# A one-core transformer layer in fp32: no tensor arithmetic on GpSimd, one-hot rows built four tokens at a time, and another order for the last layer norm

## The chip, the cores and the metric

The kernel runs on one core of a Trainium2 chip. The metric is the device time of one execution in microseconds; three runs of the kernel before gave 4892.66, 4898.55 and 4910.54 us, so the median is 4898.55 us. One further execution was recorded by the hardware profiler, and all views below come from it.

A core has five engines with instruction queues of their own: TensorE (PE; its weight loads are listed apart as PEld), VectorE (DVE), ScalarE (ACT), GpSimd (POOL) and SyncE (SP). SP computes nothing and issues transfers; ACT and POOL issue some too. Each engine works through its queue in order.

## The reference

One layer for 512 tokens of width 2048, in fp32, with three sublayers, each followed by `layer_norm(2**0.25 * x + h)`:

```
h = hybrid_mixer(x)              # mLSTM (4 heads) and forgetting attention (16 heads), gated and merged
x = layer_norm(DN_ALPHA * x + h, ln_w[0], ln_b[0])
h = memory_cross_attention(x, mem)
x = layer_norm(DN_ALPHA * x + h, ln_w[1], ln_b[1])
h = peer_ffn(x)                  # 8 heads, 16 of 16384 experts each
x = layer_norm(DN_ALPHA * x + h, ln_w[2], ln_b[2])
```

The expert sublayer matters here:

```
q = (x @ w_pq)                              # per head two halves of 128
sc = einsum(q, sub_keys)                    # 128 scores for each half
top_s, top_i = top_k(sc, 16)                # per half
cand_s = top_s[0][:, None] + top_s[1]       # 256 sums
cand_i = top_i[0][:, None] * 128 + top_i[1]
best_s, best_pos = top_k(cand_s, 16)
idx = cand_i[best_pos];  g = softmax(best_s)
a = expert_u[idx] . x                       # 128 experts per token
out = sum(gelu(a) * g * expert_v[idx])
```

## The kernel before

Every fp32 matrix product is made of three products of a split operand: a number is cast to a high half that TensorE takes at its fast fp32 rate (`hi`, by ScalarE) and the remainder (`lo = x - hi`). `split` (line 133) does this; `load_pair` (line 155) loads a weight tile of 128x1024 through SP and splits it, and `mm3`/`products` issue hi*hi, hi*lo and lo*hi. The subtraction for the low half is on VectorE, except that `load_w` (line 180) counts its loads and gives every eighth one (`work["share"] = 8`; every third one during the first sixteen steps) to GpSimd until the gates are built.

The 512 tokens go in two paths: block 0 alone (path A), then blocks 1 to 3 together (path B, 384 columns). Path A's stages run first, interleaved with other products by `weave`. The work of the expert sublayer is done in two ways. For the first 128 tokens and the last 96 tokens the chosen rows of `expert_u` and `expert_v` are fetched by indirect transfers that GpSimd issues (`gathered`), multiplied and summed by VectorE, a few steps at a time beside other stages. For the 288 tokens between them (`NDENSE`) all 16384 experts are computed densely in 128 chunks of 128 experts: `stage_a(c)` makes the chunk's activations for 288 tokens and applies gelu, `stage_h(c)` multiplies them by the chunk's gates and splits the result, and `stage_o(c0, q)` multiplies eight chunks by a quarter of `expert_v`'s columns and adds the result to an accumulator `acc` held with features on the partitions.

The gates of the dense part are a table: for each token and expert the softmax weight, or zero. It is built (lines 1245 to 1269) as a product of one-hot rows: for a token, `o1` holds a row for each of its 128 picks with a one at the second index, `o0` the same for the first index scaled by the weight, and one matmul of the two gives the token's 128x128 gates. Four tokens share a PSUM bank. ScalarE copies a bank into staging tiles (five buffers), and for each 48 tokens four transfers store these to DRAM (`gd`). `stage_h` needs the whole table. While it is built, TensorE also runs `stage_a` for the first 76 chunks (`LOOK`); most of their results wait in DRAM (`gad`).

Before the gates comes the selection (`select`, 16 calls): repeated max, index search and replacement on VectorE, with one sum and two products of 128x512 on GpSimd.

`norm` (line 743) normalises a path's rows, transposes them, applies weight and bias per feature, splits the result for the next products, transposes it back and stores it as `x2d`. The last layer norm is in `fin` (line 978): for each block of rows, statistics, then the first 1024 columns with two VectorE instructions and the other 1024 with ScalarE, GpSimd and VectorE in turn, then a store. For the dense tokens the accumulator is transposed back in quarters at the end of `stage_o`, and `2**0.25 * x` is added there from three row tiles loaded from `x2d`.

The order of the instructions on each engine, and the interleaving of independent stages on TensorE, is not written by hand: a planner lays it out when the kernel is built, from the program's order and its own estimates of durations. Rings of buffers (`bufs=`) limit how far a producer runs ahead. `after(i, other)` adds a wait to hold gathers back.

## Time and profile before

| | |
|---|---|
| median of three runs | 4898.55 us |
| profiled execution | 4901.6 us, its span 4899.9 us |
| granted TensorE clock, mean | 0.985 |
| PE busy | 4707.2 us (96%), 28705 matmuls |
| PE weight load busy | 4347.4 us (89%) |
| DVE busy | 3736.8 us (76%) |
| ACT busy | 2130.8 us (43%) |
| POOL busy | 1345.5 us (27%) |
| DMA | 1433.60 MB, mean 293 GB/s |

How to read the views: a line such as `L137 DVE TENSOR_TENSOR wlo<-raw,whi` names the line of the kernel, the engine, the operation, and what it writes from what. Where a helper issues an instruction the line is the helper's. `SPq`, `ACTq` and `POOLq` are instructions of the engine's queue that only issue or wait. A trailing `[7.94 <-DMA G<-gd]` means that the engine was idle for 7.94 us before, and that the landing of that transfer ended it. A matmul's busy time overlaps that of its neighbours, so busy sums of groups exceed the time that passes; busy time by stretch doesn't count an overlap twice.

The stages in time: path A and the products woven into it up to about 1600 us; path B's mixer, attention and cross attention up to about 2940 us; path B's last norm of this part around 2941 to 2964 us; queries and selection up to 3365 us, with `stage_a` from 3104 us; the gates from 3365 to 3661 us; the output products from 3686 to 4873 us; the last norm up to 4900 us.

### The profile page before, as it was taken

How to read it: one execution, taken by the hardware profiler on the slowest of the kernel's cores; microseconds unless marked ns; L12 is line 12 of the kernel's file. 1: busy time of each engine (PE TensorE's matmuls, PEld its weight loads, DVE VectorE, ACT ScalarE, POOL GpSimd, SP SyncE). 2: the span in 40 equal slices, each digit the busy share in tenths (PEclk: the TensorE clock that was granted, in tenths of full speed). 3: DMA queues.
4: the chain of work that ended last, by engine and by line, in shares of the span. 5: the costliest groups of instructions: out<-in, count | busy, mean ns of one | idle time of the engine just before them, and what ended most of it. 6: DMA issues, size and time to landing. Idle time of an engine off the chain costs nothing. (4 is left out here: it accounts for less than half of the span.)

```text
span 4899.9 us, 75254 instructions
## 1 busy us (share of the span) xinstructions
PE 4707.2 (96%) x28705; PEld 4347.4 (89%) x28705; DVE 3736.8 (76%) x5360; ACT 2130.8 (43%) x3108; POOL 1345.5 (27%) x1058
## 2 busy tenths in 40 slices
PE   7999999999999899999989999999998999999997
PEld 6888778878888899999988779999998999999997
DVE  7776666765698776887768585899877878888886
ACT  6665666555643322343332334434443433343333
POOL 2122222311124444434444232231111222221111
PEclk9999999999999999999999999999999999999999
DMA  7888888866559898998889584588788989989994
GB/s 259 277 290 281 290 321 311 281 226 200 193 188 357 332 358 338 342 334 328 301 297 381 192 298 164 205 281 281 282 290 325 347 339 350 345 332 348 359 336 146
DMA packets 380026, 1433.60 MB, mean 293 GB/s; under 512 B 43852, under 2 KB 104908, under 8 KB 320624
## 3 DMA queue, kind: packets, MB, share of 16 engines
q1 hardware_dynamic: 266208, 831.34, 47.9%
q0 software_dynamic: 91712, 559.45, 30.4%
q10 hardware_dynamic: 21744, 38.02, 2.1%
q8 instruction: 224, 3.67, 0.3%
q14 instruction: 138, 1.13, 0.1%
HBM read 1339.13 MB, written 89.40 MB: 292 GB/s over the span
## 5 line engine op out<-in xcount | busy, mean ns | idle before, releaser
L134 ACT CAST whi<-raw 128x1024 fp32r<-128x1024 f32 x1472 | 1526.1, 1051 | 1769.0 <-PE mm L208 780.0
L137 DVE TENSOR_TENSOR wlo<-raw,whi 128x1024 fp32r<-128x1024 f32 x1349 | 1690.3, 1265 | 711.5 <-ACT whi L134 496.2
L905 POOL DMA_INDIRECT rows<-in_peer_u,eid x224 | 327.4, 1462 | 994.6 <-DVE rows L933 352.0
L905 POOL DMA_INDIRECT rows<-in_peer_v,eid x224 | 367.4, 1640 | 837.6 <-DVE xacc L936 437.1
L208 PE MATMUL po<-hph,whi 128*128 128x288 f32 x2048 | 553.4, 297 | 33.7 <-ACT hph L134 19.5
L933 DVE SCALAR_TENSOR_TENSOR rows<-rows,xacc 128x2048 f32<-128x2048 f32 x224 | 528.0, 2361 | 71.6 <-DMA rows<-in_peer_u,eid 71.1
L936 DVE SCALAR_TENSOR_TENSOR xacc<-rows,dots,xacc 128x2048 f32<-128x2048 f32 x224 | 540.8, 2414 | 42.9 <-DMA rows<-in_peer_v,eid 41.5
L208 PE MATMUL sm<-Ch,whi 128*128 128x288 f32 x2048 | 561.3, 298 | 2.3 <-ACT whi L134 1.3
L208 PE MATMUL sm<-Cl,whi 128*128 128x288 f32 x2048 | 559.1, 297 | 0.0
L208 PE MATMUL po<-hpl,whi 128*128 128x288 f32 x2048 | 553.2, 297 | 1.9 <-DVE hpl L137 1.9
L136 POOL TENSOR_TENSOR wlo<-raw,whi 128x1024 fp32r<-128x1024 f32 x123 | 315.7, 2567 | 714.9 <-ACT whi L134 407.4
L208 PE MATMUL mm<-xh,whi 128*128 128x384 f32 x1280 | 436.7, 343 | 6.5 <-ACT sg L575 2.7
L208 PE MATMUL mm<-xl,whi 128*128 128x384 f32 x1280 | 429.4, 337 | 0.0
L208 PEld LDWEIGHTS po<-hph,whi 128*128 128x128 f32 x2048 | 385.0, 190 | 36.8 <-ACT hph L134 19.7
L208 PEld LDWEIGHTS sm<-Ch,whi 128*128 128x128 f32 x2048 | 385.4, 188 | 4.0 <-ACT whi L134 2.4
L208 PEld LDWEIGHTS po<-hpl,whi 128*128 128x128 f32 x2048 | 385.1, 190 | 3.8 <-DVE hpl L137 2.1
L208 PEld LDWEIGHTS sm<-Cl,whi 128*128 128x128 f32 x2048 | 385.6, 188 | 0.0
L208 PE MATMUL po<-hph,wlo 128*128 128x288 f32 x2048 | 339.3, 296 | 2.0 <-DVE wlo L137 2.0
L208 PE MATMUL sm<-Ch,wlo 128*128 128x288 f32 x2048 | 320.6, 297 | 0.4 <-DVE wlo L137 0.4
L208 PEld LDWEIGHTS po<-hph,wlo 128*128 128x128 f32 x2048 | 295.1, 189 | 5.2 <-DVE wlo L137 3.5
L208 PEld LDWEIGHTS sm<-Ch,wlo 128*128 128x128 f32 x2048 | 287.7, 188 | 2.4 <-DVE hpl L137 0.8
L208 PE MATMUL mm<-xh,wlo 128*128 128x384 f32 x1280 | 255.4, 335 | 0.0
(430 smaller groups left out, 8832.7 us busy)
## 6 DMA issues: line engine op xcount, KB each, us to landing
raw<-in_w_in SPq DMA_DIRECT2D x512, 512.0 KB
raw<-in_uT SPq DMA_DIRECT2D x256, 512.0 KB
raw<-in_vq SPq DMA_DIRECT2D x256, 512.0 KB
raw<-in_w_xkv SPq DMA_DIRECT2D x64, 512.0 KB
raw<-in_w_br_ml SPq DMA_DIRECT2D x64, 512.0 KB
raw<-in_w_br_fx SPq DMA_DIRECT2D x64, 512.0 KB
raw<-in_w_out SPq DMA_DIRECT2D x64, 512.0 KB
raw<-in_peer_wq SPq DMA_DIRECT2D x64, 512.0 KB
```

The source lines that it names most:

```text
L134: nc.scalar.copy(hi, src)
L136: return nc.gpsimd.tensor_sub(lo, src, hi.bitcast(F32))
L137: return nc.vector.tensor_sub(lo, src, hi.bitcast(F32))
L208: nc.tensor.matmul(o, w if stat else x, x if stat else w, start=k == first and x is xh and not part, stop=k == last and part == 1)
L905: i = nc.gpsimd.indirect_dma_start(out=rows, out_offset=None, in_=I[table], in_offset=bass.IndirectOffsetOnAxis(ap=ei[:, k:k + 1], axis=0))
L933: after(nc.vector.scalar_tensor_tensor(rows, rows, 1.0, xacc, op0=ALU.mult, op1=ALU.mult, accum_out=dots[:, k:k + 1]), last())
L936: after(nc.vector.scalar_tensor_tensor(xacc, rows, dots[:, k:k + 1], xacc, op0=ALU.mult, op1=ALU.add), last())
```

## The change

1. GpSimd computes no tensors. The low halves that it made (`share`) go to VectorE, as do the sum and the two products in `select`, and the product in `fin`, whose second 1024 columns now take the same two VectorE instructions as the first. GpSimd keeps issuing transfers and gathers.
2. Gates: both one-hot tiles are made for four tokens by one VectorE comparison each (128x512), with two buffers each; the scaling by the weight is done in place by ScalarE, one instruction of 128x128 per token.
3. `norm` for path B's second norm also stores its transposed output (288 columns of each of 16 feature tiles) to a new array `x2td`, with transfers issued from ScalarE. During the output products, each of the 16 tiles is loaded back once by SP into the ring of `gb` and added, times `2**0.25`, to the accumulator. The three row tiles of `x2d` are no longer loaded at the end.
4. The last norm of the dense tokens: after each quarter the statistics are taken from the transposed bank, and the bank is multiplied by the weight row into `yw`. At the end the root is taken for the three row tiles together. The remaining part, weight times -mean*rstd plus bias, comes from a matmul with five rows (the split weight row against the split factor, and the split bias row against ones), and one VectorE instruction per quarter and tile adds it to `yw * rstd`. Stores go out from SP and ScalarE.

```diff
-        def split(hi, lo, src, pool=False):
+        def split(hi, lo, src):
             nc.scalar.copy(hi, src)
-            if pool:
-                return nc.gpsimd.tensor_sub(lo, src, hi.bitcast(F32))
             return nc.vector.tensor_sub(lo, src, hi.bitcast(F32))
...
         def load_w(src):
-            work["n"] += 1
-            pool = work["share"] and work["n"] % work["share"] == 0
-            hi, lo, i = load_pair(src, pool)
-            if not pool:
-                work["last"] = i
+            hi, lo, work["last"] = load_pair(src)
...
                     i_last = split(*o[-1], f)
+                    if keep is not None:
+                        nc.scalar.dma_start(keep[c], f[:, :NDENSE])
...
-            nc.gpsimd.tensor_tensor(cand, vv[:, :, 0].unsqueeze(3).to_broadcast(full),
+            nc.vector.tensor_tensor(cand, vv[:, :, 0].unsqueeze(3).to_broadcast(full),
...
-                nc.gpsimd.tensor_mul(eq, eq, ii[:, :, q].unsqueeze(2).to_broadcast(full))
+                nc.vector.tensor_mul(eq, eq, ii[:, :, q].unsqueeze(2).to_broadcast(full))
...
-                o1 = gp.tile([P, 4, P], F32, tag="o1", bufs=2, name=nm("o1"))
-                nc.vector.tensor_tensor(o1, iota.unsqueeze(1).to_broadcast([P, 4, P]),
-                                        selT["i1"][:, ta:ta + 4].unsqueeze(2).to_broadcast([P, 4, P]),
-                                        op=ALU.is_equal)
+                o0, o1 = (gp.tile([P, 4, P], F32, tag=f"o{k}", bufs=2, name=nm("o")) for k in (0, 1))
+                for o, k in ((o0, "i0"), (o1, "i1")):
+                    nc.vector.tensor_tensor(o, iota.unsqueeze(1).to_broadcast([P, 4, P]),
+                                            selT[k][:, ta:ta + 4].unsqueeze(2).to_broadcast([P, 4, P]),
+                                            op=ALU.is_equal)
                 for u in range(4):
                     c = slice(ta + u, ta + u + 1)
-                    o0 = gp.tile([P, P], F32, tag="o0", bufs=4, name=nm("o0"))
-                    nc.vector.tensor_scalar(o0, iota, selT["i0"][:, c], selT["g"][:, c],
-                                            op0=ALU.is_equal, op1=ALU.mult)
-                    nc.tensor.matmul(bank[:, u * P:(u + 1) * P], o1[:, u], o0, start=True, stop=True)
+                    nc.scalar.activation(o0[:, u], o0[:, u], AF.Copy, scale=selT["g"][:, c])
+                    nc.tensor.matmul(bank[:, u * P:(u + 1) * P], o1[:, u], o0[:, u], start=True, stop=True)
...
+        def weighted(t, q, bank):
+            n, sl = size(t), slice(q * 512, (q + 1) * 512)
+            i = nc.vector.tensor_mul(yw[t][:n, sl], bank[:n], last_norm["w"][:n, sl])
+            after(i, last_norm.get("aggr"))
...
+                nc.vector.bn_stats(st[:n, t, 6 * q:6 * q + 6], bank[:n])
+                if q < 3:
+                    weighted(t, q, bank)
+                else:
+                    last_norm["aggr"] = nc.vector.bn_aggr(st[:n, t, 24:26], st[:n, t, 0:24])
+                    rest.append(bank)
...
+            rstd(st[:, :, 26], st[:, :, 25], (st[:, :, 28], st[:, :, 29]))
+            nc.vector.scalar_tensor_tensor(st[:, :, 27], st[:, :, 24], -1.0, st[:, :, 26], op0=ALU.mult, op1=ALU.mult)
+            for k in (2, 3):
+                nc.vector.tensor_copy(cs5[:, :, k], st[:, :, 27])
+            nc.vector.tensor_sub(cs5[:, :, 4], st[:, :, 27], cs5[:, :, 2].bitcast(F32))
...
+            nc.scalar.copy(l5[:5, :NDENSE], tb[:5, :NDENSE])
+            for t in range(NT):
+                weighted(t, 3, rest[t])
+            for t in range(NT):
+                n = size(t)
+                for q in range(4):
+                    sl = slice(q * 512, (q + 1) * 512)
+                    bank = sm_bank()
+                    nc.tensor.matmul(bank[:n], l5[:5, t * P:t * P + n], rw[:5, sl], start=True, stop=True)
+                    o = yw[t][:n, sl]
+                    nc.vector.scalar_tensor_tensor(o, o, st[:n, t, 26:27], bank[:n], op0=ALU.mult, op1=ALU.add)
...
-                lwd.extend(fin_load(gat))
-                for t in range(NT):
-                    n = min(P, NDENSE - t * P)
-                    xr[t] = gp2.tile([P, D], F32, tag=f"xr{t}", name=f"xr{t}")
-                    nc.gpsimd.dma_start(xr[t][:n], x2d[t + 1, :n].rearrange("p g c -> p (g c)"))
+                columns_load()
...
+            k = c0 // J
+            if 1 <= k <= 8 and q < 2:
+                b = 2 * (k - 1) + q
+                xt = mn.tile([P, NDENSE], F32, tag="gb", bufs=4, name=nm("xt"))
+                nc.sync.dma_start(xt, x2td[b])
+                nc.vector.scalar_tensor_tensor(acc[:, b], xt, ALPHA, acc[:, b], op0=ALU.mult, op1=ALU.add)
```

`columns_load` loads the weight row broadcast to all partitions, and weight and bias as single rows, splits these two and copies the halves into the five rows of `rw`, all from GpSimd's queue, when the last group of chunks begins.

More of the change, by code (lines that the diff above doesn't have):

```diff
@@ L34 @@
 GB = 48
-SHARE = 8
 NEG = -1.0e30
@@ L1013, in build @@
         A, B = Path(0, 1, XA), Path(1, 3, XB)
-        work["share"] = SHARE
         with tc.tile_pool(name="sa", bufs=1, side="right", reuse_waits="tile") as sa:
@@ L1231, in build @@
                 soften(tp, sel[t]["g"])
-        work["share"] = 0
         def o_bank(i=0):
@@ new lines, in size, with turned_out @@
+        def size(t):
+            return min(P, NDENSE - t * P)
+        def weighted(t, q, bank):
+            n, sl = size(t), slice(q * 512, (q + 1) * 512)
+            i = nc.vector.tensor_mul(yw[t][:n, sl], bank[:n], last_norm["w"][:n, sl])
+            after(i, last_norm.get("aggr"))
+        def turned_out(q):
+            st, rest = last_norm["st"], []
+            for t in range(NT):
+                n = size(t)
+                bank = o_bank()
+                for s in range(4):
+                    nc.tensor.transpose(bank[:n, s * P:(s + 1) * P], acc[:, 4 * q + s, t * P:t * P + n], ident)
+                nc.vector.bn_stats(st[:n, t, 6 * q:6 * q + 6], bank[:n])
[4 more added lines that the diff above has]
+                    rest.append(bank)
+            return rest
```

68 lines of the change are left out of this document (42 added, 26 removed).

## The prediction, made before the change was run

> **What bounds the kernel now.** I read the page's first lines, then busy time by stretch, then what TensorE waited for, then the timelines around its longest waits and at the end. In the stretch view the columns are the length and then the busy time of PE, its weight load, DVE, ACT and POOL, each with its instruction count, then the granted TensorE clock, the DMA share and GB/s.
>
> ```profile
> PE 4707.2 (96%) x28705; PEld 4347.4 (89%) x28705; DVE 3736.8 (76%) x5360; ACT 2130.8 (43%) x3108; POOL 1345.5 (27%) x1058
> ```
> ```profile
> 100.00:1600.00 1500.00, 1456.28 (x7686) 1239.67 (x7684) 1053.21 (x1626) 842.55 (x1158) 380.34 (x344) 0.99 0.77 268
> 1600.00:2900.00 1300.00, 1256.48 (x6630) 1155.87 (x6631) 986.87 (x1039) 432.93 (x629) 525.56 (x401) 0.98 0.86 322
> 2941.00:2964.00 23.00, 20.50 (x125) 18.99 (x126) 16.05 (x31) 21.56 (x42) 5.45 (x11) 0.80 0.26 104
> 3100.00:3365.00 265.00, 259.49 (x1941) 258.05 (x1940) 261.89 (x655) 110.94 (x136) 83.37 (x63) 0.99 0.77 268
> 3365.00:3667.00 302.00, 301.96 (x2367) 301.75 (x2367) 258.34 (x483) 144.75 (x400) 32.47 (x22) 1.00 0.79 283
> 3667.00:3700.00 33.00, 13.49 (x88) 13.44 (x88) 14.12 (x26) 7.04 (x14) 0.94 (x1) 0.69 0.82 292
> 4873.00:4900.00 27.00, 1.33 (x11) 0.98 (x10) 21.03 (x41) 4.33 (x6) 10.15 (x3) 0.61 0.23 87
> ```
> TensorE is the bound: 96% busy, and 302.0 of 302 us in the stretch where the gates are built. So work that is moved among VectorE, ScalarE and GpSimd costs nothing as long as TensorE keeps its operands, and a gain has to come from TensorE's holes. There are four kinds: about 44 us of holes in each of the first two long stretches (1500 less 1456.3, 1300 less 1256.5), the norm at 2941 us, where ScalarE is busy 21.6 of 23 us, the hole after 3667 us, and the end, where TensorE has nothing left and VectorE works 21 of 27 us.
>
> ```profile
> PE po L208 <- ACT hph L134: 19.5, 1, 19.5
> PE ma L208 <- POOL wlo L136: 5.0, 7, 1.3
> PE mm L208 <- POOL wlo L136: 1.9, 1, 1.9
> ```
> These are TensorE's waits: the longest of the whole run is one of 19.5 us, before the first matmul of the output products; for the low halves that GpSimd makes it waits 6.9 us altogether.
>
> **The change part by part.** *Splits.* GpSimd subtracts 123 of the 1472 low halves before; VectorE takes them.
>
> ```profile
> L137 DVE TENSOR_TENSOR wlo<-raw,whi x1349: 1161/1221/3718, 20.3 to 4856.1; 128x1024 fp32r<-128x1024 f32 x193
> L136 POOL TENSOR_TENSOR wlo<-raw,whi x123: 2355/2405/5753, 21.9 to 3092.4; 128x1024 fp32r<-128x1024 f32 x123
> L933 DVE SCALAR_TENSOR_TENSOR rows<-rows,xacc x224: 2267/2285/4822, 1475.8 to 4550.5; 128x2048 f32<-128x2048 f32 x112
> L936 DVE SCALAR_TENSOR_TENSOR xacc<-rows,dots,xacc x224: 2324/2347/5035, 2119.3 to 4758.6; 128x2048 f32<-128x2048 f32 x112
> L982 DVE SCALAR_TENSOR_TENSOR fst<-fst x6: 139/150/2290, 2910.3 to 4885.4; 128x1 f32<-128x1 f32 x3, 32x1 f32<-32x1 f32 x2, 64x1 f32<-64x1 f32 x1
> ```
> ```profile
> L137 DVE TENSOR_TENSOR wlo<-raw,whi 128x1024 fp32r<-128x1024 f32 x1349 | 1690.3, 1265 | 711.5 <-ACT whi L134 496.2
> L933 DVE SCALAR_TENSOR_TENSOR rows<-rows,xacc 128x2048 f32<-128x2048 f32 x224 | 528.0, 2361 | 71.6 <-DMA rows<-in_peer_u,eid 71.1
> L936 DVE SCALAR_TENSOR_TENSOR xacc<-rows,dots,xacc 128x2048 f32<-128x2048 f32 x224 | 540.8, 2414 | 42.9 <-DMA rows<-in_peer_v,eid 41.5
> ```
> The first fence gives min/median/max in ns, the second busy us and mean. New VectorE work: 123 x 1.221 = 150 us. But the means lie above the medians: by 44 ns for the halves, 76 ns for line 933, 67 ns for line 936, so 59 + 17 + 15 = 91 us of VectorE's busy time are not work. The L982 row shows what they are: a one-column instruction with a median of 150 ns took 2290 ns once, at 4885.4 us, while GpSimd multiplied (its row stands with the end, below). VectorE was stopped for the rest of a GpSimd instruction. So the net is 150 - 91 = +59 us, spread over 3000 us in which VectorE is 70% and 76% busy; that idle time is the cover. Bounds: 6.9 us gained if only the waits go, 59 us lost with no cover at all. I take a gain of 3 us: the waits go, and about half return as waits for a fuller VectorE. A low half is ready 1.2 us after its high half instead of 2.4 us, and GpSimd's queue of transfers and gathers no longer stands behind subtractions.
>
> The Trainium skill (SBUF — State Buffer, section "Who interferes with whom") says that a VectorE instruction with two SBUF inputs and a GpSimd instruction that reads SBUF share a read interface, and that the later one fully blocks. The trace agrees, by the 2290 ns. By that rule alone every blocked microsecond returns to VectorE; what that would be worth is the second rival.
>
> *Selection.* 48 GpSimd instructions of 128x512 go to VectorE, 27 of them between 3100 and 3365 us (18 products, 9 sums), where VectorE is busy 261.9 of 265 us.
>
> ```profile
> L847 POOL TENSOR_TENSOR eq<-eq,ixf 128x512 f32<-128x512 f32 x18 | 33.2, 1864 | 47.6 <-DVE eq L846 47.6
> L846 DVE TENSOR_TENSOR eq<-pf,iota 128x512 f32<-128x512 f32 x18 | 11.5, 678 | 0.0
> L137 DVE TENSOR_TENSOR wlo<-raw,whi 128x1024 fp32r<-128x1024 f32 x78 | 104.5, 1340 | 2.9 <-PE mm L208 2.9
> ```
> (Groups of that window alone.) VectorE does such an instruction in 0.678 us: 27 x 0.678 = 18 us more. Returned: 78 halves x (1.340 - 1.221) = 9 us. Each link of the chain shortens from 1.864 to 0.678 us. TensorE has 5.5 us of holes here. Bounds 0 to +18 us; I take +3, near the low end, since the net of 9 us falls on a TensorE with a store of low halves ahead.
>
> *Gates.* Per four tokens VectorE did one comparison of 128x512 and four of 128x128 with the scaling in them; now two of 128x512, and ScalarE scales four times.
>
> ```profile
> L1262 DVE TENSOR_SCALAR o<-iota,i0T,gT 128x128 f32<-128x128 f32 x288 | 86.5, 346 | 13.4 <-PE po L1264 13.0
> L1256 DVE TENSOR_TENSOR o<-iota,i1T 128x512 f32<-128x512 f32 x72 | 49.1, 684 | 0.0
> L1264 PE MATMUL po<-o,o x576: 270/275/377, 3365.0 to 3661.3; 128*128 128x128 f32 x192
> L1267 ACT COPY stage<-po 128x128 f32<-128x128 f32 x288 | 56.9, 279 | 67.3 <-PE po L1264 54.9 <-DMA gd<-stage 11.2 <-ACT ga L1297 0.8
> L1031 ACT ACTIVATE Ch<-sm,c_norm_w 128x128 fp32r<-128x128 f32 x16 | 5.3, 363 | 0.0
> ```
> ```profile
> 3662.33 2.75 ACTq L1269 DMA_DIRECT2D gd<-stage  x3
> ```
> ```profile
> 3681.25 0.61 SPq L1309 DMA_DIRECT2D G<-gd  x1
> ```
> ```profile
> 3685.56 0.83 DVE L1327 TENSOR_TENSOR ga<-ga,G 128x288 f32<-128x288 f32 x2 [7.94 <-DMA G<-gd]
> ```
> VectorE: 4 x 0.346 + 0.684 = 2.07 us becomes 2 x 0.684 = 1.37 us, 0.70 us less, 50 us over 72 groups. ScalarE: 288 scalings at most 0.363 us (line 1031, the nearest row, also a 128x128 scaling by a column) = 105 us on top of 144.8, 250 of 302 us: still under TensorE. TensorE does the same work. What matters is when the gates end. They run from 3365.0 to 3661.3 us, 4.17 us a group, mixed with first products from the look-ahead of 76 chunks. Their last stores are issued until 3665.1, the load of the first gates goes out at 3681.25 when these have landed, VectorE gets them at 3685.56, and TensorE, out of products since 3667.0, waits. If the gates end 19.5 us sooner (0.27 us a group of 4.17), products remain to cover the landing. VectorE's 0.70 us a group is more than twice that, and the scaled rows now have two buffers of four tokens instead of four of one, so the next group no longer waits for the last matmul of this one. The later start (the net of 9 us above) leaves 50 - 9 = 41 us. I take the hole as closed: -19 us. Bounds: -21 us (with the slow clock behind it: 13.5 us of matmuls at a granted 0.69) to +16 us, if each scaling took 0.60 us and ScalarE with 144.8 + 173 = 318 us became the bound of this stretch; it decides from 0.545 us on.
>
> The Trainium skill (ScalarE: Activation LUTs, "Rules for kernel authors") speaks against this part: multiplications belong on VectorE. Its figures (186 ns, 93 ns for a column operand, 0.833 ns an element, 93 ns overlap) give an estimate of 0.293 us each, 84 us in all, which leads to the same sum.
>
> *Norm store.* Sixteen transfers are issued from ScalarE in the norm at 2941 us, whose ScalarE is full.
>
> ```profile
> 4712.58 0.33 ACTq L1299 DMA_DIRECT2D gad<-ga  x1
> 4713.00 2.94 ACT L134 CAST whi<-raw 128x1024 fp32r<-128x1024 f32 x3 [0.45 <-ACT ga L1297]
> ```
> The same size of transfer, issued from ScalarE elsewhere, holds its next instruction back by 0.45 us; 16 x 0.45 = 7.2 us. TensorE has only the norm's transposes there. Bounds 0 to 12 (7.2, and 5 more if the ring of six staging tiles waits for landings); I take +6. *The 16 loads and additions* of x in the output products: VectorE 16 x 0.45 = 7 us over 1100 us at 80%, SyncE 16 issues among the weights: 0, or 7 with no cover. *The gathered blocks' last norm*: two VectorE instructions of about 1.3 us replace one and a GpSimd product, under running matmuls: 0.
>
> *The end.*
>
> ```profile
> 2939.42 0.17 DVE L252 TENSOR_SCALAR rst<-rst 128x3 f32<-128x3 f32 x1
> 2940.88 0.17 DVE L740 SCALAR_TENSOR_TENSOR rst<-rst 128x3 f32<-128x3 f32 x1
> ...
> 4872.14 1.55 DVE L1367 TENSOR_TENSOR acc<-acc,po 128x288 f32<-128x288 f32 x4 [6.52 <-PE po L208]
> 4874.15 1.87 DVE L1375 SCALAR_TENSOR_TENSOR xr<-xr,po 128x512 f32<-128x512 f32 x3 [0.46 <-PE po L1373]
> 4875.95 1.86 DVE L976 BATCH_NORM_STATS2 fst<-xr 128x6 f32<-128x512 f32 x3
> 4877.74 0.48 DVE L980 BATCH_NORM_AGGREGATE fst<-fst 128x2 f32<-128x24 f32 x3
> 4892.25 4.47 DVE L992 TENSOR_TENSOR xr<-xr,lw 128x1024 f32<-128x1024 f32 x2 [2.24 <-POOL xr L991]
> ```
> ```profile
> 4884.35 10.15 POOL L991 TENSOR_TENSOR xr<-xr,lw 128x1024 f32<-128x1024 f32 x3 [81.87 <-ACT xr L990]
> ```
> Now: last accumulation done at 4873.7, residual 1.9, statistics 1.9, then scaling in three engines, held up by GpSimd's 10.15 us; the last VectorE instruction ends at 4896.7. After: the residual is already in, statistics can start at 4874.15 and take 1.9 + 0.5 us, the root for three tiles 1.6 us (2939.42 to 2941.05), four small instructions 0.7, transposes, a copy and a first matmul 1.9 (three handovers), meanwhile the three weighted quarters, then 12 x 0.62 us = 7.4 (0.62 = 1.87/3, the same instruction on PSUM). That ends at 4888.2, 8.5 us sooner; I take -8. Bounds -10 to 0 (a late weight row would take it all).
>
> **Sum.** -3 + 3 - 19 + 6 + 0 + 0 - 8 = -21 us. The profiled execution took 4901.6 us (its span is 4899.9), so 4880.6; it lies 3.05 us over the median of the three runs, 4898.55, so 4877.5.
>
> **The rivals.** (1) *The hole stays*, because the order of gates and products is laid down by a planner and the gates may be paced by their stores (five staging tiles; 11.2 us of line 1267's waits are for them) rather than by VectorE. For it: the pace of 4.17 us is twice VectorE's 2.07. Then -2 us: 4896.5. (2) *The holes of the first 2900 us shrink* because VectorE is no longer stopped at random. Of 87 us, a quarter (my choice; no row splits the holes by this cause): -22 more, 4855.5. Against it: TensorE waits for GpSimd only 6.9 us by the row. (3) *VectorE becomes the bound* where it is nearly full: the net of the splits, 59 us, and of the selection, 48 x 0.678 less 9 = 24 us, together 83 us, comes uncovered by two thirds, +55: 4932.5, and 4960.5 if all of it. It decides from the point where TensorE's waits for low halves pass 21 us more than now. For it: 261.9 of 265 us; against it: 70% and 76% elsewhere.
>
> **How the numbers follow.** Forecast 0.48, own range 4866 to 4890; rival 1 0.22, rival 2 0.15, rival 3 0.15. Half a per cent, 24.5 us, is about what a measurement can tell from no change: faster is below 4874.1, slower above 4923. Faster: rival 2 and nearly half of the forecast, 0.38. Slower: nearly all of rival 3, 0.13. Same: rival 1 and the other half of the forecast, 0.49. The range leaves out rival 3 and the far side of rival 2, under 0.2 together: 4850 to 4914.
>
> **What would show it.** TensorE's longest wait (19.5 us for the first high half of a gate product) gone, or under 5 us; the last gate matmul at least 20 us before the first output product; the mean of the low halves at 1.22 us; the norm at about 2941 us longer by 6 us in ScalarE's column; from the last accumulation to the end 18 us instead of 26. The prediction is wrong if that wait remains, if TensorE waits for VectorE's low halves by tens of us, or if ScalarE is full while gates are built.

## The result and the profile after

The kernel after takes 4830.32 us (median of 4 runs, 4827.06 to 4833.53) against 4900.31 us for the kernel before, run beside it. The ratio is 0.9859, 95% interval 0.9842 to 0.9877, that is 69 us less (60 to 77). Forecast were 4877.5 us, with a range from 4850 to 4914: the gain is some three times the one predicted, and outside the range.

The profiled execution took 4827.06 us, its span is 4825.3 us. The first two fences are the page's line of busy times and the stretches that answer to those shown of before (same columns). The stretches begin and end at about the same landmarks as there, so they lie earlier; the other products that TensorE mixes into them differ (1941 matmuls before the gates and 2367 beside them in before, 2235 and 1792 here).

```profile
PE 4695.9 (97%) x28720; PEld 4343.2 (90%) x28720; DVE 3736.9 (77%) x5326; ACT 2203.7 (46%) x3388; POOL 932.2 (19%) x884
```
```profile
100.00:1570.00 1470.00, 1445.20 (x7677) 1238.44 (x7676) 1074.13 (x1717) 846.77 (x1159) 162.43 (x254) 0.99 0.80 274
1570.00:2861.00 1291.00, 1251.51 (x6627) 1152.01 (x6626) 993.23 (x1074) 432.14 (x625) 431.36 (x367) 0.99 0.87 324
2902.30:2925.30 23.00, 20.46 (x124) 18.90 (x125) 15.96 (x30) 21.80 (x42) 5.35 (x10) 0.80 0.56 207
3065.00:3363.00 298.00, 297.02 (x2235) 296.55 (x2236) 287.63 (x704) 127.81 (x160) 52.09 (x40) 1.00 0.82 281
3363.00:3590.00 227.00, 226.02 (x1792) 225.53 (x1792) 177.19 (x225) 189.67 (x644) 23.01 (x14) 1.00 0.78 277
3590.00:3625.00 35.00, 35.00 (x266) 35.00 (x265) 20.42 (x26) 14.38 (x22) 4.76 (x3) 1.00 0.97 365
4806.00:4827.00 21.00, 8.77 (x21) 3.20 (x18) 13.49 (x31) 0.60 (x2) 0.00 (x0) 0.57 0.30 113
```
TensorE's holes in the first stretch are 1470 less 1445.2, 24.8 us, where before had 43.7; in the second 39.5 against 43.5. The stretch of the gates took 227 us in place of 302, and the hole behind it is gone: 35.0 of 35 us busy. The norm, 23 us, is as long as before. VectorE's sum hardly moved (3736.9 against 3736.8 us), GpSimd's fell from 1345.5 to 932.2.

To see where 74.6 us of span went, one takes places that both kernels have. These are the instructions of a tile's group, before and then after; behind the colon stand min/median/max in ns and the first and last start.

```profile
L208 PE MATMUL mm<-xh,whi x1280: 333/334/737, 899.7 to 2468.6; 128*128 128x384 f32 x183
L208 PE MATMUL sm<-Ch,whi x2048: 289/295/442, 3103.8 to 4801.8; 128*128 128x288 f32 x187
L208 PE MATMUL po<-hph,whi x2048: 288/294/609, 3686.5 to 4871.0; 128*128 128x288 f32 x187
L208 PE MATMUL po<-hph,wlo x2048: 288/295/442, 3690.6 to 4872.2; 128*128 128x288 f32 x187
```
```profile
L201 PE MATMUL mm<-xh,whi x1280: 333/334/737, 868.2 to 2435.2; 128*128 128x384 f32 x183
L201 PE MATMUL sm<-Ch,whi x2048: 289/296/407, 3065.2 to 4734.1; 128*128 128x288 f32 x187
L201 PE MATMUL po<-hph,whi x2048: 288/294/442, 3617.7 to 4803.9; 128*128 128x288 f32 x187
L201 PE MATMUL po<-hph,wlo x2048: 288/295/442, 3619.8 to 4804.7; 128*128 128x288 f32 x187
```

| place | after less before | gained up to it since the last place |
|---|---|---|
| first product of the second path's first head (899.7) | -31.5 | 31.5 |
| first look-ahead product (3103.8) | -38.6 | 7.1 |
| first output product (3686.5) | -68.8 | 30.2 |
| last output product (4872.2) | -67.5 | -1.3 |
| end of the span (4899.9) | -74.6 | 7.1 |

So 30 us were gained where the selection and the gates stood, where the prediction had 16 (19 less 3), and 7 at the end (8 there). What was not forecast are 31 us in the first 900 us, where the diff touches only the shared low halves. The experiments are about these, and about the terms one by one. "The place" is from here on the first row of the table: 899.7 us in before. Four experiments below (gates, tail, selection, and the gates' scaling on VectorE) keep before's code and its order of instructions beyond that place, and they put it at 895.2, 889.7, 893.5 and 895.5, so a single profile can lie 5 us off. Their mean with before is 894.7. TensorE has done the same work up to the place in every run (4776 to 4782 matmuls). But the planner lays the instructions out anew when the low halves move, so that the order in after differs from before's from 25 us on VectorE and 48 us on TensorE; this is in all numbers on the low halves and was not separated from the edits.

### The profile page after: what moved, and what is told of

It reads as the page before. It is cut to its first block, busy times and chain, and to the rows that moved or that the text cites. A ratio compares the mean times of both kernels' runs of the same rounds, so it can differ in the third digit from the quotient of the medians.

```text
span 4825.3 us, 75381 instructions
## 1 busy us (share of the span) xinstructions
PE 4695.9 (97%) x28720; PEld 4343.2 (90%) x28720; DVE 3736.9 (77%) x5326; ACT 2203.7 (46%) x3388; POOL 932.2 (19%) x884
## 5 line engine op out<-in xcount | busy, mean ns | idle before, releaser
L134 DVE TENSOR_TENSOR wlo<-raw,whi 128x1024 fp32r<-128x1024 f32 x1472 | 1782.0, 1220 | 746.3 <-ACT whi L133 512.9
L932 DVE SCALAR_TENSOR_TENSOR xacc<-rows,dots,xacc 128x2048 f32<-128x2048 f32 x224 | 525.4, 2345 | 21.6 <-DMA rows<-in_peer_v,eid 20.1
L929 DVE SCALAR_TENSOR_TENSOR rows<-rows,xacc 128x2048 f32<-128x2048 f32 x224 | 511.3, 2285 | 24.1 <-DMA rows<-in_peer_u,eid 23.2
L201 PEld LDWEIGHTS mm<-xh,whi 128*128 128x128 f32 x1280 | 242.2, 189 | 14.3 <-ACT whi L133 4.5
```

The source lines that it names most:

```text
L134: return nc.vector.tensor_sub(lo, src, hi.bitcast(F32))
L201: nc.tensor.matmul(o, w if stat else x, x if stat else w, start=k == first and x is xh and not part, stop=k == last and part == 1)
L929: after(nc.vector.scalar_tensor_tensor(rows, rows, 1.0, xacc, op0=ALU.mult, op1=ALU.mult, accum_out=dots[:, k:k + 1]), last())
L932: after(nc.vector.scalar_tensor_tensor(xacc, rows, dots[:, k:k + 1], xacc, op0=ALU.mult, op1=ALU.add), last())
```

## The experiments

**One part at a time.** Four kernels are the kernel before with one part of the diff each.

```
-            pool = work["share"] and work["n"] % work["share"] == 0
+            pool = False                       # low halves on VectorE alone
```


> Kernel before, with the one edit that GpSimd makes none of the weights' low halves; VectorE makes them all. The traces of before and after part by 31 us between 340 and 900 us of the span, where the shared low halves are the only thing that the diff touches. Theory S (the sharing itself costs the time, by the raw buffer that GpSimd holds longer or by VectorE standing still beside it): the whole run is 31 to 40 us shorter than before, and the fox branch of the first path begins some 30 us earlier. Theory O (the 31 us are an accident of the order that the planner lays out once all edits are in): this kernel is within 10 us of before. My prediction's own term for this edit was -3.

Measured 0.9919 (0.9905 to 0.9932) of before: 40 us less (33 to 47). The place came at 868.3 us, as in after (its order of instructions is that of after up to 1329 us), the look-ahead 32.1 us and the end of the span 34.2 us earlier than in before: by the profiles nearly all of the gain of this edit lies in the first 900 us. Page line and longest wait of this kernel:

```profile
PE 4693.5 (96%) x28705; PEld 4347.5 (89%) x28705; DVE 3769.2 (77%) x5483; ACT 2136.0 (44%) x3107; POOL 1021.8 (21%) x935
```
```profile
PE po L208 <- ACT hph L134: 18.9, 1, 18.9
```
The wait ahead of the output products is still there. VectorE is busy 32 us more than before, not the 59 forecast; yet that was no loss. Theory S holds.

```
-                o1 = gp.tile(...); nc.vector.tensor_tensor(o1, iota, selT["i1"], op=ALU.is_equal)
+                o0, o1 = ...; the same comparison for "i0" and "i1", 128x512 each
                 for u in range(4):
-                    nc.vector.tensor_scalar(o0, iota, selT["i0"][:, c], selT["g"][:, c], is_equal, mult)
+                    nc.scalar.activation(o0[:, u], o0[:, u], AF.Copy, scale=selT["g"][:, c])
```


> Kernel before, with the edit of the gates' one-hot rows alone. Theory G (the gates' stage alone made the wait of 19.5 us ahead of the output products, and its pace falls from 4.17 to about 3.1 us a group whatever GpSimd does): 17 to 25 us shorter than before, last gate matmul at least 20 us ahead of the first output product. Theory L (the stage got faster because GpSimd no longer works beside it): less than 10 us shorter, pace above 3.7 us.

Measured 0.9966 (0.9952 to 0.9979): 17 us less (10 to 24). In its profile the gates' products read

```profile
L1263 PE MATMUL po<-o,o x576: 270/275/378, 3376.0 to 3589.5; 128*128 128x128 f32 x192
```
The pace is (3589.5 - 3376.0) / 71 = 3.01 us a group against 4.17, with GpSimd's selections and halves as before, and the wait of 19.5 us is no longer among the waits. The last gate product lies 84.7 us ahead of the first output product (3674.2). Theory G holds, with the gain at its low edge.

```
+                    if keep is not None:
+                        nc.scalar.dma_start(keep[c], f[:, :NDENSE])
 ...  and with it the 16 loads and additions, the weighted quarters and the five rows
```


> Kernel before, with the last norm's part alone: the norm's extra store from ScalarE, the 16 loads and additions beside the output products, the weighted quarters and the five rows at the end. From the trace of after, the end after the last accumulation is 7 us shorter and the norm with the store is not longer: 6 to 9 us shorter than before. By my prediction's terms (store +6, end -8): 2 us shorter. Rival (the loads and additions delay the output products): 0 to 10 us longer.

Measured 0.9998 (0.9989 to 1.0008): 1 us less, from 5 less to 4 more. The profiled span is 6.8 us shorter (4893.1), all of it behind the last output product; the norm with its stores lost nothing against before, the output products nothing. So the one profile shows a gain, the runs cannot tell it from none, and the 6 to 9 us expected lie outside their interval: that expectation missed.

```
-            nc.gpsimd.tensor_tensor(cand, ...)      -                nc.gpsimd.tensor_mul(eq, ...)
+            nc.vector.tensor_tensor(cand, ...)      +                nc.vector.tensor_mul(eq, ...)
```


> Kernel before, with the selection of the best keys on VectorE alone. The trace of before has TensorE idle for 3.85 us at one place and some 5 us in all in this stage; my prediction's term was +3 (0 to +18). Theory L (GpSimd's two operations in the chain are slow and stop VectorE): 5 to 10 us shorter than before. Theory V (VectorE gets two more operations for each of the 16 selections and becomes late): 3 to 18 us longer.

Measured 0.9991 (0.9982 to 1.0000): 4 us less (0 to 9): theory V, 3 to 18 us longer, falls; theory L's 5 to 10 us shorter is neither reached by the mean nor excluded. In its profile the first gate product starts 23 us later than in before, though the look-ahead starts 13.9 us earlier, and still the wait ahead of the output products shrank:

```profile
PE po L208 <- ACT hph L134: 14.6, 1, 14.6
```
The four parts sum to 62 us; the whole is 69 (60 to 77). The two products of GpSimd in the gathered blocks' norms were not run alone.

**Why the low halves cost 31 us.** Three things differ when GpSimd makes a low half: VectorE stands still beside it, the raw buffer comes free later, and TensorE gets the half later. The next kernels are the kernel after with one of them put back, for the same loads that before shared.

```
+        def burden(i, src):                          # i: the high half's cast
+            after(nc.gpsimd.tensor_sub(dum, dum, dum), i)       # 128x512, scratch, twice
+            nc.gpsimd.tensor_sub(dum, dum, dum)
```


> Kernel after, and beside it, for the same loads that before shared (each third, later each eighth, up to the end of the first path's products with the memory), GpSimd subtracts as many elements (2 x 128 x 512) of a scratch tile once the load's high half is made. VectorE still makes every low half, so no raw buffer waits for GpSimd. Place to read: the first product of the second path's first head, 899.7 us in before and 868.2 in after. Theory K (VectorE standing still beside GpSimd's subtractions costs the time): that place comes 15 to 30 us later than in after, VectorE's subtractions take longer than 1.22 us in the mean there. Theory R (the raw buffer held by GpSimd costs it): within 5 us of after.

The place came at 880.3 us, 12 us later than in after; the whole run at 0.9882 (0.9860 to 0.9904). Theory R allowed 5, theory K wanted 15 or more: neither holds. Groups between 340 and 865 us:

```profile
L137 DVE TENSOR_TENSOR wlo<-raw,whi 128x1024 fp32r<-128x1024 f32 x261 | 343.0, 1338 | 122.9 <-ACT whi L134 108.6 <-PE ma L210 9.0 <-PE mm L210 2.2
L165 POOL TENSOR_TENSOR dum<-dum 128x512 f32<-128x512 f32 x32 | 53.0, 1657 | 145.6 <-ACT whi L134 132.1 <-ACT Ch L1041 9.5 <-ACT p L661 4.0
L166 POOL TENSOR_TENSOR dum<-dum 128x512 f32<-128x512 f32 x32 | 51.6, 1612 | 2.0
```
VectorE's halves take 1.338 us in the mean against 1.223 in after, so VectorE does stand still. 12 us is rather too much for it: GpSimd is at it 3.27 us for each shared load here and 2.4 in before, and VectorE's halves lose 30 us (261 x 0.115) here where they lost 21 in before (222 of them, 1.316 us in the mean against the median of 1.221).

```
             i = split(hi, lo, raw)
+            if hold:
+                nc.gpsimd.memset(raw, 0.0)          # raw is free only when this is done
```


> Kernel after, and beside it, for the loads that before shared, GpSimd overwrites the raw tile once VectorE has read it. The raw buffer comes free only when GpSimd is through, as in before; GpSimd reads no tensor. Theory R (the held raw buffer makes the next weight load late): the first product of the second path's first head comes 15 to 35 us later than the 868.2 us of after, whole run 20 to 45 us longer than after, the subtractions of VectorE as short as in after (1.22 us). Theory K (VectorE standing still): within 5 us of after there, unless the subtractions of VectorE are longer.

The place came at 865.2 us, 3 us earlier than in after. Theory R, that the held raw buffer is the cause, falls as far as the place goes. The same stretch:

```profile
L135 DVE TENSOR_TENSOR wlo<-raw,whi 128x1024 fp32r<-128x1024 f32 x262 | 315.7, 1223 | 148.2 <-ACT whi L134 132.9 <-PE ma L207 7.1 <-PE mm L207 3.4
L161 POOL MEMSET raw<- 128x1024 f32 x33 | 32.4, 981 | 151.0 <-DVE wlo L135 107.0 <-DMA raw<-in_w_in 20.1 <-DMA raw<-in_w_br_ml 16.6
```
The overwriting takes 0.98 us more after VectorE's 1.22, and it does not slow VectorE: 51 of VectorE's halves in the run overlap one, and they too take 1.223 us. The whole run is at 0.9885 (0.9863 to 0.9906), some 13 us longer than after; 8 of the 12 us in the profiled executions arise behind 3600 us, where the code is that of after, and I cannot explain them.

```
+            pool, bufs = ring["pool"], ring["raw"]
+            if ring is W and fourth:
+                fourth[0] += 1
+                if fourth[0] % 4 == 0:
+                    pool, bufs = w0, 1            # one raw tile more
```


> Kernel before with GpSimd's low halves kept, and one raw buffer more (the first ring has four in place of three) up to the end of the first path's products with the memory. Theory R: that place (899.7 us in before) comes 15 to 35 us earlier, and the waits of SyncE's queue for low halves fall. Theory K: within 6 us of before.

Every fourth load of the first ring uses the added tile, up to the end of the first path's products with the memory; to make room, three other tiles were made smaller or shared, and one ring of small tiles has three in place of four in the first path. In the kernel before, with GpSimd's halves kept, this moved the place to 868.8 us:

```profile
L213 PE MATMUL mm<-xh,whi x1280: 331/334/737, 868.8 to 2445.8; 128*128 128x384 f32 x183
```
That is 31 us, or 26 from the mean, as much as the edit of the halves brought at the place. The whole run gained less, 0.9967 (0.9956 to 0.9978), 16 us against that edit's 40; 9 of the 31 us were lost again up to the look-ahead. Theory K expected 6 at most. But the mechanism that theory R gave is not the right one either: the waits of SyncE's queue for low halves did not fall. They are 367.7 us in this kernel (340 to 868 us) against 356.5 in before (340 to 900 us):

```profile
SPq L153 <- DVE wlo L137: 311.3, 201, 6.9
SPq L153 <- POOL wlo L136: 56.4, 24, 4.6
```
```profile
SPq L148 <- DVE wlo L137: 293.0, 194, 6.7
SPq L148 <- POOL wlo L136: 63.5, 26, 5.5
```


> Kernel after, with one raw buffer more over the same stretch. The waits of ScalarE for raw tiles in that stretch (340 to 900 us) were some 134 us in before and 62 in after, so under theory R some of it is left to win: the place (868.2 us in after) comes 3 to 15 us earlier. If the loads themselves (312 GB/s in that stretch) are the bound by now: within 3 us of after. Theory K says nothing here.

The same buffer in the kernel after: place at 850.7 us, 17.5 us earlier, more than the 15 that theory R allowed. The whole run, 0.9835 (0.9815 to 0.9854) of before, 4819.39 us, is the fastest kernel measured here; its profiled span is 14.6 us under that of after. So the buffer does not make GpSimd's halves free: with it on both sides the kernel without them is still 18 us ahead at the place (850.7 against 868.8), and the whole change is worth 65 us (0.9835 against 0.9967) where it was worth 69 without. Of the 26 to 31 us the buffer hides 8 to 13, and the rest of what it brings is a gain of its own. What the buffer changes is seen in the stretch up to the place, in before, after and this kernel (length, PE, PEld, DVE, ACT, POOL, clock, DMA share, GB/s):

```profile
340.00:899.00 559.00, 533.80 (x2999) 454.73 (x2998) 357.34 (x409) 342.62 (x501) 155.09 (x162) 0.99 0.86 301
```
```profile
338.00:868.00 530.00, 520.69 (x2978) 449.79 (x2977) 366.95 (x442) 342.13 (x499) 74.36 (x129) 1.00 0.91 317
```
```profile
332.00:850.00 518.00, 515.19 (x2968) 449.90 (x2967) 367.29 (x441) 343.42 (x497) 74.20 (x129) 1.00 0.91 323
```
and in what ScalarE's casts waited for there, in before and in after; in the third kernel no wait for a load is among the three longest:

```profile
ACT whi L134 <- DMA raw<-in_w_in: 70.0, 44, 5.3
```
```profile
ACT whi L133 <- DMA raw<-in_w_in: 36.9, 28, 3.3
```
```profile
L133 ACT CAST whi<-raw 128x1024 fp32r<-128x1024 f32 x266 | 277.6, 1054 | 143.3 <-PE mm L206 78.2 <-PE ma L206 52.6 <-DVE wlo L134 5.2
```
TensorE's holes go 25.2, 9.3, 2.8 us: I read this as loads that come just in time in before, so that the cast of a high half, its low half and the products follow each other with nothing in hand. Part of the lost time is no hole: between 340 us and the place the granted clock fell to half twice in before, for 3 us each time, and never in after, which is worth 3.4 us.

```
+            if twice:
+                nc.gpsimd.tensor_sub(dum, raw, hi)      # as before's, into a bf16 scratch tile
```


> Kernel after, and beside it, for the loads that before shared up to the end of the first path's products with the memory, GpSimd makes the low half a second time, from the same raw tile and high half, into a scratch tile that nobody reads. So VectorE stands still beside it as in before and the raw buffer is held as in before; only the low half that TensorE waits for comes early, from VectorE. Place to read: the first product of the second path's first head, 868.2 us in after, 880.3 with GpSimd on a scratch tile alone, 899.7 in before (893 to 900 over the four kernels with its code there). Theory RK (hold and standstill together, while the loads are just in time, make the loss): 20 to 30 us later than in after. Theory D (the late low half itself is what more than half of the loss comes from): 5 to 14 us later.

The place came at 915.5 us, 47 us later than in after and 16 later than in before: beyond both theories. The whole run is at 0.9952 (0.9936 to 0.9968), some 46 us longer than after. The rows show why it does not separate them:

```profile
L135 DVE TENSOR_TENSOR wlo<-raw,whi 128x1024 fp32r<-128x1024 f32 x253 | 350.2, 1413 | 124.7 <-ACT whi L134 116.3 <-PE ma L207 2.7 <-PE mm L207 2.2
L161 POOL TENSOR_TENSOR dum<-raw,whi 128x1024 bf16<-128x1024 f32 x31 | 91.3, 2946 | 159.7 <-ACT whi L134 145.9 <-issue 13.7
```
Both engines subtract the same load at the same moment; VectorE's mean rises to 1.413 us and GpSimd's to 2.95, so the half that TensorE waits for is late here too.

```
+                late[0] = nc.gpsimd.memset(raw, 0.0)
 ...
-                        nc.tensor.matmul(o, ...)
+                        j = nc.tensor.matmul(o, ...);  if part: after(j, late[0])
```


> Kernel after with the raw tile overwritten by GpSimd once VectorE has read it, for the loads that before shared (that alone left the place at 865.2 us), and now TensorE's products with the low half of such a load wait for that overwriting too, so that the low half comes some 1.2 us late for TensorE, without GpSimd reading a tensor. Theory D (the late low half): the place comes 10 to 20 us later than 865.2 us, the whole run 15 to 40 us longer than that kernel. Theory RK: within 5 us of it.

The place:

```profile
L208 PE MATMUL mm<-xh,whi x1280: 331/334/737, 883.4 to 2460.1; 128*128 128x384 f32 x183
```
It came 18 us later than with the overwriting alone, 15 later than in after; whole run 0.9916 (0.9894 to 0.9937), 15 us longer than with the overwriting alone. Theory D holds, theory RK falls, though the order of instructions differs between the two from 134 us on. (In the profile some 16 us more than in after are lost up to the look-ahead, where each eighth load still is late; before lost 7 there, but so did the kernel with the overwriting alone, 8.) And yet TensorE's direct waits for that instruction, 340 to 865 us, are

```profile
PE ma L208 <- POOL raw L161: 1.5, 3, 0.6
```
Where the other 14 to 17 us went can be followed a part of the way. Between 340 us and the place, with the overwriting alone and then with the late half, the stretch and ScalarE's longest wait for loads are

```profile
340.00:865.00 525.00, 514.96 (x2935) 443.05 (x2933) 362.25 (x436) 335.33 (x487) 104.70 (x160) 1.00 0.90 315
ACT whi L134 <- DMA raw<-in_w_in: 49.0, 36, 3.1
```
```profile
340.00:883.00 543.00, 524.82 (x2972) 452.29 (x2970) 366.08 (x439) 340.18 (x499) 105.75 (x162) 0.99 0.89 309
ACT whi L134 <- DMA raw<-in_w_in: 52.3, 26, 4.6
```
TensorE's holes rise from 10.0 to 18.2 us, and all but 1.5 of these 8 us lie in front of products with high halves, not with late low ones. The clock costs 3.4 us more, and 7 us were behind already at 340 us (37 matmuls more are left to do from there). ScalarE's wait for loads rises by 3.3 us only.

Last, this late half together with the one raw buffer more:

> Kernel after with the low halves late for TensorE as in the kernel that left the place (first product of the second path's first head) at 883.4 us, and the one raw buffer more that brought it from 868.2 to 850.7 us without the late halves. Theory A (a deeper ring lets the high halves be made ahead of TensorE, so that a late low half is hidden): the place within 5 us of 850.7. Theory N (the late low half is paid whatever the ring, and the buffer's gain is another one that adds to it): 862 to 868 us.

The place came at 856.5 us, so the late halves cost 5.8 us and not 15 to 18; whole run 0.9868 (0.9852 to 0.9885), 24 us less than without the buffer. That misses theory A's bound by 0.8 us and theory N's by 5.5; since a single profile can be 5 us off, it speaks for theory A without settling it. By these places the deeper ring hides some two thirds of what the late halves cost.

**The gates' scaling on VectorE.**

```
+                nc.vector.tensor_mul(o0, o0, selT["g"][:, ta:ta + 4] broadcast over 128)
                 for u in range(4):
-                    nc.scalar.activation(o0[:, u], ...)
```


> Kernel before, the gates' one-hot rows four tokens at a time, but scaled by VectorE in one multiplication of 128 x 512 and not by ScalarE. VectorE's time a group is that of before by the rows: 3 x 0.685 = 2.06 us against 0.684 + 4 x 0.346 = 2.07. Theory V (VectorE's own time sets the stage's pace, and the gain comes from handing work to ScalarE): within 5 us of before, pace near 4.17 us a group, the wait ahead of the output products stays. Theory H (the hand-overs between VectorE and TensorE, five in a group, set it): 12 to 25 us shorter, as with ScalarE.

Measured 0.9984 (0.9971 to 0.9997): 8 us less (1 to 14), between the theories.

```profile
L1260 DVE TENSOR_TENSOR o<-o,gT x72: 679/684/689, 3367.9 to 3642.7; 128x512 f32<-128x512 f32 x72
L1262 PE MATMUL po<-o,o x576: 270/275/377, 3368.7 to 3646.7; 128*128 128x128 f32 x192
```
```profile
PE po L208 <- ACT hph L134: 7.0, 1, 7.0
```
With VectorE's time unchanged (3 x 0.684 us a group) the pace is (3646.7 - 3368.7) / 71 = 3.92 us and the wait 7.0 us in place of 19.5. So fewer hand-overs, with the larger buffers that come with them, bring 12.5 of the 19.5 us of the wait, though only 0.25 of the 1.16 us of pace; the rest of the pace comes from the move to ScalarE.

## Why the prediction was wrong

**The splits (-3, bounds -7 to +59).** This is the step that failed; measured alone it is -40 (-47 to -33). The working priced GpSimd's slow halves by TensorE's direct waits for them, 6.9 us, and made that the best case: "6.9 us gained if only the waits go". A wait row names only what came last at one matmul. The experiments show that late halves cost some ten times what their row says: 1.5 us of direct waits, 15 to 18 us at the place. The rest is booked elsewhere, as holes in front of later products with high halves. ScalarE's waits for loads fell with the lost time (70.0 in before, 36.9 in after, none among the first with the added buffer), which suggests a delay passed on from the products to the next cast, raw buffer and load; but the overwriting alone raised these waits from 36.9 to 49.0 us and lost no time at the place, and the late half, which lost 18 us, raised them by 3.3 more. So that chain is not borne out, and how a late half delays later high halves stays open. The second thing is VectorE's standstill, at most 12 us in the same stretch. The raw buffer's later release alone cost nothing measurable at the place. That late halves and standstill simply add up to before's 26 to 31 us is not shown, only that each has such a price, in single profiles and with another order of instructions. One raw buffer more takes 9 to 12 us off the late halves' price (5.8 us left); of GpSimd's halves as a whole 18 us are left with it.

**Where it applies.** The prediction spread the effect over 3000 us. It sits in the first 900, and I read this from the pace: there TensorE has 128 rows of activations for a tile of weights and needs a new tile every 2 us. The casts from 340 to 865 us in before, and then from 340 to 865 us and from 1600 to 2900 us in after, are

```profile
L134 ACT CAST whi<-raw 128x1024 fp32r<-128x1024 f32 x252 | 260.5, 1053 | 176.6 <-DMA raw<-in_w_in 69.4 <-PE ma L208 28.4 <-PE mm L208 27.5
```
```profile
L133 ACT CAST whi<-raw 128x1024 fp32r<-128x1024 f32 x264 | 273.6, 1053 | 162.7 <-PE mm L201 54.6 <-DMA raw<-in_w_in 36.9 <-PE ma L201 36.8
L133 ACT CAST whi<-raw 128x1024 fp32r<-128x1024 f32 x275 | 289.0, 1053 | 664.1 <-PE mm L201 547.3 <-DMA raw<-in_w_out 30.2 <-issue 28.0
```
525 / 264 = 1.99 us a tile, against 1300 / 275 = 4.73 us. A half that takes 2.4 us after a cast of 1.05 us fits the second and not the first. The numbers for this were in the trace of before, 252 casts in 525 us or 2.08 us each, and the prediction did not divide them. The pace is not the whole reason: from 100 to 340 us before needs a tile every 1.97 us too and GpSimd made 15 of the 122 low halves, yet the 1800th matmul, at 342 us, is only 4.5 us later than in after. So what makes the price so high after 340 us is open.

**Rival 2** (holes of the first 2900 us shrink by a quarter, -22, chance 0.15) was nearest. Holes did shrink, by 18.9 us in the first stretch, nearly half, and by 4.0 in the second. But its cause, VectorE stopped at random, carries the smaller part by the runs on after, 12 against 15 to 18 us; and its counter-argument, the 6.9 us, was the row that misled. A further 11 us of the first stretch are not holes: TensorE's busy time for nearly the same work (7686 and 7677 matmuls) fell from 1456.3 to 1445.2 us. Matmul ends are modelled in the profile, and what these 11 us were is open.

**VectorE's own time.** The rule of the Trainium skill (SBUF — State Buffer, "Who interferes with whom") was told right and weighed wrongly. In after the halves read

```profile
L134 DVE TENSOR_TENSOR wlo<-raw,whi 128x1024 fp32r<-128x1024 f32 x1472 | 1782.0, 1220 | 746.3 <-ACT whi L133 512.9
```
1.220 us in the mean, as announced; the two operations of 128x2048 have means of 2285 and 2345 ns, the medians of before within 2 ns. With the halves alone the net was 32 us and not 59. Rival 3 (VectorE becomes the bound) found nothing: TensorE's wait list in after has no row of VectorE's weight halves among its first.

**Selection (+3).** -4 (-9 to 0) alone. But the way there was mis-sized: the first gate product comes 297.9 us behind the look-ahead's first in after and 261.2 in before, 37 us later where the net of VectorE's time was put at 9. It costs nothing, since TensorE works on look-ahead products meanwhile (297.0 of 298 us busy; the holes of 5.5 us went) and the gates make it up.

**Gates (-19).** Right: -17 (-24 to -10) alone, in after the longest wait gone and the last gate product at 3581.6, 36 us ahead of the output products. One size in it was off without harm: the pace fell from 4.17 to (3581.6 - 3363.1) / 71 = 3.08 us a group, more than the 0.70 us of VectorE's time, which by the run with the scaling on VectorE is not the whole mechanism. (The bound of -21 is not what the prediction's own figures give: 19.5 + 0.31 x 13.5 = 23.7.) The scalings read

```profile
L1250 PE MATMUL po<-o,o x576: 270/275/377, 3363.1 to 3581.6; 128*128 128x128 f32 x192
```
```profile
L1249 ACT ACTIVATE o<-o,gT 128x128 f32<-128x128 f32 x288 | 94.3, 424 | 19.6 <-DVE o L1244 16.4 <-issue 3.2
```
A record lasts 0.424 us in the mean, longer than the 0.363 taken as the bound, but neighbours overlap: the 288 fill 94.3 us, under the 105 of the bound and over the 84 of the estimate. Where one scaling follows another directly they start 0.293 us apart (median), as in the estimate worked out from the Trainium skill's figures (ScalarE: Activation LUTs). ScalarE did not become the bound (189.7 of 227 us busy). Rival 1, that the stores pace the gates, falls.

**Norm store (+6).** Measured 0: the norm has the same 23 us, ScalarE 21.80 us busy against 21.56. In after's timeline the transfers are issued beside ScalarE's running instructions (ACTq marks what the queue issues):

```profile
2909.96 0.59 ACT L766 COPY ra<-mm 128x512 f32<-128x512 f32 x1
2910.39 0.33 ACTq L762 DMA_DIRECT2D x2td<-t  x1
2910.44 0.59 ACT L766 COPY ra<-mm 128x512 f32<-128x512 f32 x1
```
The next copy starts 0.48 us after the one before, with the issue between them. Of the 16 issues one has a gap of 0.14 us behind it, one a gap that waits for TensorE, the others none. The row taken for the price (0.45 us) is right for its own place and wrong for this one: in before the next instruction comes 0.40 us or more behind all 108 Gelus of line 1297 that such a store follows, and within 0.03 us behind 21 of the 26 that none follows. There the store has to wait for the result of the instruction just ahead of it, and in the norm its tile was made earlier, so the low end, 0, was the right value.

**The end (-8).** -7 by the profiles, though the runs of that part alone do not show it: from the last accumulation's end to the end of the span 19.3 us in place of 26.2.

```profile
4804.78 1.18 DVE L1422 TENSOR_TENSOR acc<-acc,po 128x288 f32<-128x288 f32 x3 [5.77 <-PE po L201]
4806.42 1.88 DVE L1359 BATCH_NORM_STATS2 st<-po 128x6 f32<-128x512 f32 x3 [0.46 <-PE po L1358]
...
4814.27 7.98 DVE L1390 SCALAR_TENSOR_TENSOR yw<-yw,st,sm 128x512 f32<-128x512 f32 x12 [2.09 <-PE sm L1388]
```
Twelve last steps took 7.98 us for the 7.4 forecast, the hand-overs ahead of them 2.1 for 1.9. The 16 loads and additions cost at most the 1.3 us of the table.

**The sum** of the parts outside the splits was -18; the runs give 4 + 17 + 1 = 22 alone and the places 36 together. The 37 us that the splits' term missed are most of the 47 by which 4877.5 was too high.

## What to carry to other kernels

Do not price a slow producer by the waits that name it: here the rows said 6.9 us and taking the producer out brought 40. Divide the stretch by its tiles: where the time for one tile is shorter than the producer's latency and the casts wait for loads, suspect that the rows show a small part, and measure it with the one edit alone. One load buffer more is cheap to try and was worth some 16 us in before and 11 in after; it hid two thirds of what late halves alone cost, but it did not replace the edit. An engine's mean above its median was the sign of a standstill here, but the price is read at the engine that bounds the kernel.

## What the runs showed of the hardware

GpSimd subtracting in SBUF slowed VectorE's two-input subtraction (1.338 against 1.223 us in the mean, 1.627 for the 124 that overlap one of GpSimd's in that run), GpSimd only writing did not (1.223), for the same loads. The Trainium skill (SBUF — State Buffer, "Who interferes with whom") says this of instructions that read SBUF and those that only write it; the rows agree. A subtraction of 128x1024 takes GpSimd 2.4 us and VectorE 1.22; two of 128x512 took GpSimd 3.27, so two halves were dearer there than one whole, each time beside a working VectorE.
